# A two-layer diffusion trunk: channel sums of the last output tiles, idle products at the broadcasts, and the order of the residual update

## The chip, the cores and the metric

One core of one Trainium2 chip runs the whole program. The metric is the device time of one execution in microseconds, as the median of several runs.

## The reference

The model has two layers, and each layer three sublayers: a SwiGLU feed-forward, a token mixer with four branches, and a second feed-forward. There are 384 tokens (128 of a prompt, 256 latent ones) with 1024 channels. Every sublayer has the same frame, and the change lies in that frame:

```python
def trunk_layer(x, mod, lp, layer_idx, cache):
    h = modulate(x, lp["norm_pre"][0], mod[:, 0], mod[:, 1])
    x = residual_add(x, swiglu(h, lp["ffn_in"][0], lp["ffn_out"][0]), lp["norm_post"][0], mod[:, 2], 0.5)
...
def modulate(x, g_pre, shift, scale):
    return rms_norm(x, g_pre) * (1.0 + scale[:, None, :]) + shift[:, None, :]

def residual_add(x, y, g_post, gate, weight):
    return x + weight * gate[:, None, :] * rms_norm(y, g_post)
```

So at the end of a sublayer the mean of y^2 over the channels is needed for the update of x, and the mean of the new x^2 over the channels for the input h of the next sublayer. All arithmetic is float32.

## The kernel before

Channels lie on the partitions, tokens in the free dimension: x is eight tiles (KD = 8) of 128 channels by 384 tokens. Every float32 weight and activation is split into a rounded part and a rest (`split`, line 959: a CAST on ScalarE and a subtraction on VectorE or POOL), and each product is three products of the parts (`acc3`, lines 955 to 957). Weights come by DMA from SP into a ring of three and are split on arrival (`weight`).

A sublayer ends with eight output tiles. `out_evac` (line 991) takes each out of PSUM. Let c be the factor of a channel (weight, gate and norm_post together, one for the prompt's and one for the latent tokens, GRP). It makes y^2 (line 995, ScalarE, from PSUM), c y (line 1002, the tile `yp` or, in a mixer, `room`), (c y)^2 and x c y. The three squares and products are added over the tiles into `acc`, on POOL, some on VectorE in a mixer (line 1009). For tile 7 it makes x c y and (c y)^2 in two pieces directly from PSUM (lines 999 and 1000) and leaves them outside `acc`.

`sums` (line 1011) sums over the 128 channels of a tile on TensorE: a product with a column of ones, one per block of 128 tokens, nine for three tiles of 384 tokens. One such call takes `acc` (tiles 0 to 6) ahead of the last products of tile 7, another one, in `post_stats` (line 1020), the three tiles of tile 7. VectorE adds the two parts; `mp` (line 1033) is the mean of y^2, and POOL raises it to the power -1/2 (`qp`, line 1035). From the other sums, qp and the running mean of x^2, the mean of the new x^2 follows without a look at the new x (lines 1044 to 1048), and its power `qn` on POOL (line 1051).

`next_h` (line 1054) brings qp and qn to all partitions by three products each with the identity (`bcast`, line 968: Rp and Rn in PSUM), and then takes the eight tiles in turn: yp times Rp (line 1064), x plus that (line 1066, on VectorE for tile 0, on POOL for the others), xn = x times Rn (line 1074), h from xn on ScalarE in two pieces (line 1080), and its split. The first two weights of the next sublayer are loaded and split ahead (`self.early`); the second's rest (`lin`) is made in two halves by `rest` (line 945), whose place is fixed with `behind`, a dependency that only orders.

Beside this, products of the modulation's rows (line 855, "mod-row products": four products of 2 by 256 for each of eight row blocks) are placed there; `rows_gate` in `run` says behind which broadcast each block may stand. In the mixer the whole sublayer including its output tiles is recorded, and an order is computed by a planner with assumed costs (`Order`); it is emitted at line 1305, with idle products of a zero tile `wsrc` at line 1288 in TensorE's planned gaps. Outside the mixers the tile framework sets the order.

## Time and profile before

| what | us |
|---|---|
| median of 3 runs | 1970.43 |
| lowest and highest run | 1960.71, 1972.06 |
| the profiled execution, its time | 1969.64 |
| the profiled execution, its span | 1967.6 |
| TensorE busy in the span | 1885.2 |
| VectorE busy | 1230.4 |
| ScalarE busy | 825.4 |
| POOL busy | 428.4 |

The span goes from the first to the last instruction in the trace; the time of the execution holds some 2 us around it. In the rows below PE is TensorE's products, PEld its loading of weights, DVE is VectorE, ACT is ScalarE, POOL is GpSimd. A row of the timeline gives the start, the length, the engine, the line, the operation with the tiles it writes and reads, their shapes, how many equal instructions are merged, and in brackets how long the engine had waited and for whom. A float32 product of TensorE counts as two in the trace.

### The profile page before, as it was taken

Reading aid. Unit: us, or ns where it says so; the run is one execution under the profiler, and the core shown is the slowest. Engines: PE = TensorE matmul, PEld = TensorE weight load, DVE = VectorE, ACT = ScalarE, POOL = GpSimd, SP = SyncE. Lnnn points to the kernel's source line nnn. Section 1 sums busy time; section 2 is a strip of 40 time slices with the busy share of each in tenths; the row PEclk is TensorE's granted clock in tenths of the full one; section 3 lists DMA queues with packets and bytes.
Section 4 is the critical chain, followed back from the end, with each engine's and each line's share of the span. In section 5 each row is a group of like instructions: output and inputs, shape, how many; then the busy total and the mean of one; then the engine's idle time right before and its main releaser. Section 6 shows DMA issues by size and latency. Waiting matters only on the chain.

```text
span 1967.6 us, 36586 instructions
## 1 busy us (share of the span) xinstructions
PE 1885.2 (96%) x14962; PEld 1737.7 (88%) x14962; DVE 1230.4 (63%) x2272; ACT 825.4 (42%) x1463; POOL 428.4 (22%) x364
## 2 busy tenths in 40 slices
PE   6999999999999999999999999999999999999997
PEld 3989998888787879999979999978987778899997
DVE  3797476686678558635758735757866775433344
ACT  3433333565245453333353333344543544533332
POOL 0111132240100231121431111424100014222223
PEclk9999999989899989999999999999898999999999
DMA  9676454233231238635538644533333222333442
GB/s 368 204 245 209 142 189 159 97 90 90 70 98 60 97 117 278 200 124 162 162 137 276 205 129 154 170 104 95 83 95 77 84 91 81 102 125 124 126 125 91
DMA packets 118519, 277.15 MB, mean 141 GB/s; under 512 B 46416, under 2 KB 51792, under 8 KB 117968
## 3 DMA queue, kind: packets, MB, share of 16 engines
q1 hardware_dynamic: 70704, 252.75, 39.5%
q10 hardware_dynamic: 47648, 22.07, 4.5%
q8 instruction: 117, 1.92, 0.4%
q14 instruction: 50, 0.41, 0.1%
HBM read 266.92 MB, written 7.86 MB: 140 GB/s over the span
## 4 chain that ended last, share of the span: by engine, by line
PE 74%; DVE 13%; ACT 4%; issue 4%; DMA 3%; POOL 1%; ACTq 0%; DVEq 0%; POOLq 0%
PE psum L1305 23%; PE psum L956 16%; PE psum L957 16%; PE psum L955 16%; DVE room L1305 5%; DVE mj L822 3%; DVE lin L961 1%; ACT room L1305 1%; DMA mw<-in_wmod 1%; PE psum L1016 1%; DVE wlo L1305 1%; PE psum L968 1%; ACT whi L1305 1%; ACT h L1080 1%; DMA rfo<-in_ffn_out 1%
## 5 line engine op out<-in xcount | busy, mean ns | idle before, releaser
L957 PE MATMUL psum<-h,lin 128*128 128x384 f32 x1408 | 474.8, 337 | 13.3 <-DVE lin L961 13.3
L956 PE MATMUL psum<-h,hin 128*128 128x384 f32 x1408 | 475.6, 338 | 2.0 <-DVE h L961 1.5
L955 PE MATMUL psum<-h,hin 128*128 128x384 f32 x1408 | 470.0, 337 | 2.6 <-ACT h L960 2.0
L960 ACT CAST hin<-rin 128x1024 fp32r<-128x1024 f32 x175 | 183.9, 1052 | 401.7 <-PE psum L956 266.6
L961 DVE TENSOR_TENSOR lin<-rin,hin 128x1024 fp32r<-128x1024 f32 x175 | 217.2, 1242 | 175.1 <-ACT hin L960 175.1
L957 PEld LDWEIGHTS psum<-h,lin 128*128 128x128 f32 x1408 | 265.3, 188 | 19.6 <-DVE lin L961 19.4
L956 PEld LDWEIGHTS psum<-h,hin 128*128 128x128 f32 x1408 | 265.3, 188 | 9.0 <-DVE h L961 8.9
L961 POOL TENSOR_TENSOR hl<-hf,hh 128x384 fp32r<-128x384 f32 x88 | 137.7, 1564 | 613.9 <-ACT hh L960 613.9
L955 PEld LDWEIGHTS psum<-h,hin 128*128 128x128 f32 x1408 | 263.2, 188 | 7.5 <-ACT h L960 4.2
L822 DVE SCALAR_TENSOR_TENSOR mj<-mw,sr 128x1024 f32<-128x1024 f32 x176 | 250.8, 1425 | 16.4 <-DMA mw<-in_wmod 10.3
L1305 PE MATMUL psum<-room 32*32 32x32 f32 (+10 forms) x5112 | 241.8, 232 | 8.0 <-DVE room L1305 4.5
L1305 PEld LDWEIGHTS psum<-room 32*32 32x32 f32 (+5 forms) x5112 | 193.5, 132 | 56.6 <-issue 18.6
L957 PE MATMUL psum<-hh,lfo 128*128 128x384 f32 x704 | 237.6, 338 | 2.8 <-DVE lfo L961 2.8
L955 PE MATMUL psum<-hh,hfo 128*128 128x384 f32 x704 | 237.7, 338 | 1.9 <-ACT hfo L960 1.8
L956 PE MATMUL psum<-hl,hfo 128*128 128x384 f32 x704 | 236.9, 337 | 0.0
L1305 PE MATMUL psum<-h,whi 128*128 128x384 f32 x736 | 201.0, 353 | 6.3 <-ACT whi L1305 6.0
L960 ACT CAST hfo<-rfo 128x1024 fp32r<-128x1024 f32 (+1 forms) x96 | 94.1, 980 | 232.6 <-PE psum L956 167.2
L961 DVE TENSOR_TENSOR lfo<-rfo,hfo 128x1024 fp32r<-128x1024 f32 (+1 forms) x96 | 111.1, 1157 | 120.5 <-ACT hfo L960 120.5
L1009 POOL TENSOR_TENSOR acc<-acc,t 128x384 f32<-128x384 f32 x72 | 105.9, 1497 | 231.7 <-ACT t L995 231.7
L1305 PEld LDWEIGHTS psum<-h,whi 128*128 128x128 f32 x736 | 137.9, 196 | 11.0 <-ACT whi L1305 7.9
L957 PEld LDWEIGHTS psum<-hh,lfo 128*128 128x128 f32 x704 | 132.7, 188 | 4.9 <-DVE lfo L961 4.6
L955 PEld LDWEIGHTS psum<-hh,hfo 128*128 128x128 f32 x704 | 132.7, 189 | 3.2 <-ACT hfo L960 3.2
(189 smaller groups left out, 2508.7 us busy)
## 6 DMA issues: line engine op xcount, KB each, us to landing
rin<-in_ffn_in SPq DMA_DIRECT2D x176, 512.0 KB, 3.6
mw<-in_wmod SPq DMA_DIRECT2D x88, 512.0 KB, 4.6
rfo<-in_ffn_out SPq DMA_DIRECT2D x64, 512.0 KB, 3.6
wraw<-in_w_in SPq DMA_DIRECT2D x46, 512.0 KB, 3.6
rfo<-in_ffn_out SPq DMA_DIRECT2D x32, 384.0 KB, 3.2
m<-in_wmodk SPq DMA_DIRECT2D x16, 512.0 KB, 9.5
ma<-in_wmodk SPq DMA_DIRECT2D x16, 512.0 KB, 4.6
wraw<-in_w_out SPq DMA_DIRECT2D x16, 512.0 KB, 3.7
```

The source lines that it names most:

```text
L822: i = nc.vector.scalar_tensor_tensor(junk, w, 1.0, self.sr[:, c], op0=ALU.mult, op1=ALU.mult, accum_out=self.mod[l][:, part, j, c : c + 1])
L955: nc.tensor.matmul(ps, w, xh, start=first, stop=False)
L956: nc.tensor.matmul(ps, w, xl, start=False, stop=False)
L957: nc.tensor.matmul(ps, wl, xh, start=False, stop=last)
L960: return (self.nc.scalar.copy(hi, src), (engine or self.nc.vector).tensor_tensor(lo, src, hi.bitcast(F32), op=ALU.subtract))
L961: (engine or self.nc.vector).tensor_tensor(lo, src, hi.bitcast(F32), op=ALU.subtract))
L968: i = self.nc.tensor.matmul(ps[:, b * P : (b + 1) * P], r[:, b : b + 1].to_broadcast([P, P]), self.k("ident"), start=True, stop=True)
L1009: (nc.vector if (m, i) in quick else nc.gpsimd).tensor_tensor(acc[i], acc[i], t3[i], op=ALU.add)
L1016: self.summed = self.nc.tensor.matmul(st[:, 3 * i + b : 3 * i + b + 1], part[i][:, b * P : (b + 1) * P], self.k("ones")[:, 0:1], start=Tru ...
L1080: nc.scalar.activation(h[:, o : o + n], xn[:, o : o + n], AF.Identity, bias=B[:, j, g : g + 1], scale=A[:, j, g : g + 1])
L1305: getattr(getattr(nc, eng), n["fn"])(*args, **kw)
```

## The change

For tiles 6 and 7 `out_evac` now makes only y^2 (ScalarE) and x*y (VectorE, from PSUM over all 384 tokens), both without c. The factors come in where the channels are summed: the weight column is c for x*y, and for y^2 a pair of columns, 1 and c^2 (`w2`, made in `post_coef`), so that one product gives the sum of y^2 and that of (c y)^2. `acc` ends with tile 5. All sums go into the same nine columns of PSUM. The first call takes `acc` and tile 6, the second tile 7. At the end of the program only the sum of y^2 is taken. `warm` puts eight idle products behind the sums and, between two broadcasts, eight more. In `next_h` the update of tile j+1 (yp, x) stands ahead of xn of tile j, and the second half of `lin` behind the split of tile 1. `rows_gate` lets fewer row blocks stand ahead of the second broadcast.

```diff
@@ post_coef
+        self.w2 = self.one(f"w2{l}_{s}", [2, 2, 2], tag="w2", bufs=2)
+        nc.gpsimd.memset(self.w2[:, :, :, 0], 1.0)
+        nc.vector.tensor_tensor(self.w2[:, :, :, 1], c[:, KD - 2 :], c[:, KD - 2 :], op=ALU.mult)
@@ out_evac
+        late = m >= KD - 2
...
-        if m == KD - 1:
-            for g, (o, n) in enumerate(GRP):
-                nc.vector.scalar_tensor_tensor(t3[1][:, o : o + n], ps[:, o : o + n], c(g), self.x[:, m, o : o + n], op0=ALU.mult, op1=ALU.mult)
-                nc.scalar.activation(t3[2][:, o : o + n], ps[:, o : o + n], AF.Square, scale=c(g))
+        if late:
+            nc.vector.tensor_tensor(t3[1], self.x[:, m], ps, op=ALU.mult)
...
-                (nc.vector if (m, i) in quick else nc.gpsimd).tensor_tensor(acc[i], acc[i], t3[i], op=ALU.add)
+                nc.gpsimd.tensor_tensor(acc[i], acc[i], t3[i], op=ALU.add)
@@ sums
+    def sum_tile(self, st, m, t3, coef, only):
+        mm, stop = self.nc.tensor.matmul, False
+        both = st.rearrange("p (i b) -> p i b", b=3)[:, ::2]
+        for b in range(3):
+            g, blk = min(b, 1), slice(b * P, (b + 1) * P)
+            if only:
+                self.summed = mm(st[:, b : b + 1], t3[0][:, blk], self.k("ones")[:, 0:1], start=False, stop=m == KD - 1 and b == 2)
+            else:
+                mm(both[:, :, b], t3[0][:, blk], self.w2[:, m - KD + 2, g], start=False, stop=stop)
+        if not only:
+            for b in range(3):
+                g, blk = min(b, 1), slice(b * P, (b + 1) * P)
+                self.summed = mm(st[:, 3 + b : 4 + b], t3[1][:, blk], coef[:, m, g : g + 1], start=False, stop=m == KD - 1 and b == 2)
+
+    def warm(self, n):
+        ps = self.bank([P])
+        for _ in range(n):
+            self.behind(self.nc.tensor.matmul(ps, self.wsrc[:, :P], self.wsrc[:, :P], start=True, stop=True), self.gates[-1])
+        self.pf(ps)
@@ post_stats
-        for i in range(n):
-            nc.vector.tensor_scalar(cut(st, i), cut(acc[0], i), scale[i], 0.0 if i else EPS, op0=ALU.mult, op1=ALU.add)
-        st2 = self.sums(acc[1], n)
+        self.sum_tile(ps, KD - 1, t3, coef, last)
...
+        self.warm(8)
...
-        now = nc.vector.scalar_tensor_tensor(mp, cut(st2, 0), scale[0], cut(st, 0), op0=ALU.mult, op1=ALU.add)
+        now = nc.vector.tensor_scalar(mp, cut(ps, 0), 1.0 / D, EPS, op0=ALU.mult, op1=ALU.add)
@@ next_h
+        if Rp is not None and rn is not None:
+            self.warm(8)
...
+            if Rp is not None and (j == 0 or Rn is None):
+                ahead = step(j)
+            if Rp is not None and Rn is not None and j < KD - 1:
+                ahead = step(j + 1)
...
+            i = nc.vector.tensor_tensor(xn, self.x[:, j], Rn, op=ALU.mult)
+            if Rp is not None:
+                self.behind(i, ahead)
...
+            if Rp is not None and j == 1:
+                self.rest(self.made[1])
@@ run
-                self.rows_gate = {k: self.gates[(k + 1) // 2 - 1 if k < 7 else 2] for k in range(1, KD)}
+                self.rows_gate = {k: self.gates[0 if k == 1 else 1 if k < 4 else 2] for k in range(1, KD)}
@@ mix_out
-            t3 = self.out_evac(f"m{l}", m, ps, coef, yp, acc, ((5, 2), (6, 1), (6, 2)))
+            t3 = self.out_evac(f"m{l}", m, ps, coef, yp, acc)
```

TensorE's order at the end of the first mixer, before: the sums (128x1) of `acc`, then those of tile 7, the mod-row products (2x256) between them, and the broadcasts of qp and qn.

```order
L1305 MATMUL psum<-consts,room_2980 128x1 x9
L855 MATMUL psum<-room_2980,sc 2x256 x2
L1016 MATMUL psum<-consts,t_6855 128x1 x3
L855 MATMUL psum<-room_2980,sc 2x256 x2
L1016 MATMUL psum<-consts,t_6860 128x1 x3
L1016 MATMUL psum<-consts,t_6865 128x1 x3
L855 MATMUL psum<-room_2980,sc 2x256
L968 MATMUL psum<-consts,qp_6902 128x128 x3
L855 MATMUL psum<-room_2980,sc 2x256 x4
L968 MATMUL psum<-consts,qn_6913 128x128 x3
L855 MATMUL psum<-room_2980,sc 2x256 x23
```

The same place now, up to the first of the eight idle products (each is a LDWEIGHTS and a MATMUL of `wsrc`):

```order
L1335 MATMUL psum<-consts,room_2990 128x1 x9
L1335 MATMUL psum<-w_1_3007,t_6868 128x2 x3
L1335 MATMUL psum<-co_1_3006,t_6874 128x1 x3
L1029 MATMUL psum<-w_1_3007,t_6888 128x2 x3
L1033 MATMUL psum<-co_1_3006,t_6893 128x1 x3
L1039 LDWEIGHTS wsrc
L1039 MATMUL psum<-wsrc 128x128
```

And from the last idle product ahead of the second broadcast to the next sublayer's first products:

```order
L1039 LDWEIGHTS wsrc
L1039 MATMUL psum<-wsrc 128x128
L971 MATMUL psum<-consts,qn_6949 128x128 x3
L855 MATMUL psum<-room_2990,sc 2x256 x32
L958 MATMUL psum<-h_6965,hin_0_6909 128x384
```

The 21 sums now stand in one row, and all 32 mod-row products stand behind the second broadcast. After a feed-forward sublayer four of them stay ahead of the sums of tile 7 and 28 stand behind, where 23 stood.

VectorE's order in the first `next_h` behind a sublayer, before: yp is yp times Rp, `lin` the halves of the second early weight's rest, the row `h<-h` the split of tile 0.

```order
L1064 TENSOR_TENSOR yp_0_1957<-yp_0_1957,psum 128x384
L945 TENSOR_TENSOR lin_1_2818<-rin_1_2816,hin_1_2817 128x512
L1066 TENSOR_TENSOR x<-x,yp_0_1957 128x384
L945 TENSOR_TENSOR lin_1_2818<-rin_1_2816,hin_1_2817 128x512
L1074 TENSOR_TENSOR xn_0_2861<-x,psum 128x384
L1064 TENSOR_TENSOR yp_0_1957<-yp_0_1957,psum 128x384
L1064 TENSOR_TENSOR yp_1_1958<-yp_1_1958,psum 128x384
L1074 TENSOR_TENSOR xn_1_2870<-x,psum 128x384
```

Now:

```order
L1085 TENSOR_TENSOR yp_0_1960<-yp_0_1960,psum 128x384
L948 TENSOR_TENSOR lin_1_2818<-rin_1_2816,hin_1_2817 128x512
L1087 TENSOR_TENSOR x<-x,yp_0_1960 128x384
L1085 TENSOR_TENSOR yp_0_1960<-yp_0_1960,psum 128x384
L1100 TENSOR_TENSOR xn_0_2872<-x,psum 128x384
L1085 TENSOR_TENSOR yp_1_1961<-yp_1_1961,psum 128x384
L1100 TENSOR_TENSOR xn_1_2881<-x,psum 128x384
L1085 TENSOR_TENSOR yp_1_1961<-yp_1_1961,psum 128x384
L1100 TENSOR_TENSOR xn_2_2891<-x,psum 128x384
L964 TENSOR_TENSOR h_2867<-h_0_2873,h_2867 128x384
L1085 TENSOR_TENSOR yp_2_1962<-yp_2_1962,psum 128x384
L964 TENSOR_TENSOR h_2867<-h_1_2882,h_2867 128x384
```

A tile `yp_n` holds two of the eight tiles. The update of tile 1 moved ahead of xn_0, and the second half of `lin` from there to behind the split of tile 1 (it is the next row).

## Rows read from the trace of the kernel before

**Rows 1.** The page: busy time by engine, and the chain that ended last.

```profile
PE 1885.2 (96%) x14962; PEld 1737.7 (88%) x14962; DVE 1230.4 (63%) x2272; ACT 825.4 (42%) x1463; POOL 428.4 (22%) x364
...
PE 74%; DVE 13%; ACT 4%; issue 4%; DMA 3%; POOL 1%; ACTq 0%; DVEq 0%; POOLq 0%
```

**Rows 2.** Timeline, third place, 999 to 1011 us (start, length, engine, line, operation).

```profile
999.76 0.34 PE L957 MATMUL psum<-hh,lfo 128*128 128x384 f32 x1
...
1000.20 0.49 ACT L995 ACTIVATE t<-psum 128x384 f32<-128x384 f32 x1 [4.32 <-PE psum L957]
...
1000.80 0.35 DVE L999 SCALAR_TENSOR_TENSOR t<-psum,co,x 128x128 f32<-128x128 f32 x1 [2.46 <-ACT t L995]
...
1004.65 0.93 PE L968 MATMUL psum<-consts,qp 128*128 128x128 f32 x6 [0.67 <-POOL qp L1035]
...
1005.62 0.56 DVE L1064 TENSOR_TENSOR yp<-yp,psum 128x384 f32<-128x384 f32 x1 [0.24 <-PE psum L968]
...
1006.09 0.68 DVE L945 TENSOR_TENSOR lin<-rin,hin 128x512 fp32r<-128x512 f32 x1
...
1006.36 1.65 PE L968 MATMUL psum<-consts,qn 128*128 128x128 f32 x6
...
1006.69 0.55 DVE L1066 TENSOR_TENSOR x<-x,yp 128x384 f32<-128x384 f32 x1
...
1007.16 0.69 DVE L945 TENSOR_TENSOR lin<-rin,hin 128x512 fp32r<-128x512 f32 x1
...
1008.05 0.56 DVE L1074 TENSOR_TENSOR xn<-x,psum 128x384 f32<-128x384 f32 x1 [0.20 <-PE psum L968]
...
1010.19 0.55 DVE L1074 TENSOR_TENSOR xn<-x,psum 128x384 f32<-128x384 f32 x1 [0.66 <-POOL x L1066]
```

**Rows 3.** Windows, E to xn_0 at five places: length, busy times by engine, PEclk, DMA.

```profile
332.91:341.66 8.75, 7.70 (x61) 4.87 (x64) 3.92 (x14) 2.89 (x6) 1.72 (x2) 0.80 0.11 47
698.65:711.11 12.46, 12.14 (x71) 8.48 (x73) 4.79 (x19) 2.89 (x6) 1.71 (x2) 0.63 0.10 38
1000.10:1008.05 7.95, 6.79 (x52) 4.59 (x56) 4.01 (x14) 2.89 (x6) 1.71 (x2) 0.85 0.11 46
1297.11:1305.08 7.97, 6.81 (x53) 4.60 (x56) 4.00 (x14) 2.89 (x6) 1.71 (x2) 0.85 0.12 50
1659.50:1670.55 11.05, 10.73 (x71) 7.49 (x73) 4.79 (x19) 2.89 (x6) 1.71 (x2) 0.73 0.10 40
```

**Rows 4.** Windows, E to mp at the same five places.

```profile
332.91:336.67 3.76, 3.07 (x28) 2.36 (x28) 0.84 (x3) 2.19 (x6) 0.00 (x0) 1.00 0.27 109
698.65:705.73 7.08, 7.01 (x46) 5.56 (x45) 1.62 (x8) 2.89 (x6) 0.00 (x0) 0.73 0.18 67
1000.10:1003.50 3.40, 2.91 (x27) 2.28 (x28) 0.84 (x3) 2.19 (x6) 0.00 (x0) 1.00 0.27 107
1297.11:1300.51 3.40, 2.91 (x28) 2.29 (x28) 0.84 (x3) 2.19 (x6) 0.00 (x0) 1.00 0.29 117
1659.50:1665.17 5.67, 5.60 (x46) 4.57 (x45) 1.62 (x8) 2.84 (x6) 0.00 (x0) 0.94 0.19 77
```

**Rows 5.** Timeline of TensorE: sums, mod-row products, sums behind the first mixer, idle products.

```profile
327.62 2.07 PE L1016 MATMUL psum<-consts,acc 128*128 128x1 f32 x18
...
341.14 2.77 PE L855 MATMUL psum<-ma,sc 128*2 128x256 f32 x46
...
702.97 2.72 PE L1016 MATMUL psum<-consts,t 128*128 128x1 f32 x12
...
1320.72 0.62 PE L1288 MATMUL psum<-wsrc 128*128 128x128 bf16 x8
```

**Rows 6.** Windows, 703 to 710 us, behind the first mixer (columns as in rows 3).

```profile
703.00:710.00 7.00, 6.75 (x32) 4.73 (x31) 2.38 (x10) 1.36 (x3) 1.71 (x2) 0.50 0.01 2
```

**Rows 7.** Timeline: TensorE's waits in and behind the eight tiles of a next sublayer.

```profile
716.19 0.19 PEld L956 LDWEIGHTS psum<-h,hin 128*128 128x128 f32 x1 [0.40 <-DVE h L961]
...
1024.93 0.44 PE L957 MATMUL psum<-h,lin 128*128 128x384 f32 x1 [0.82 <-DVE lin L961]
```

More of the change, by code (lines that the diff above doesn't have):

```diff
@@ L1008, in out_evac, with sums @@
             for i in range(3):
-                (nc.vector if (m, i) in quick else nc.gpsimd).tensor_tensor(acc[i], acc[i], t3[i], op=ALU.add)
-    def sums(self, part, n=3):
+                nc.gpsimd.tensor_tensor(acc[i], acc[i], t3[i], op=ALU.add)
+    def sums(self, acc, t3, coef, only):
         st = self.bank([9])
-        for i in range(n):
+        for i in range(1 if only else 3):
             for b in range(3):
-                self.summed = self.nc.tensor.matmul(st[:, 3 * i + b : 3 * i + b + 1], part[i][:, b * P : (b + 1) * P], self.k("ones")[:, 0:1],
-                                                    start=True, stop=True)
-        return st
+                self.nc.tensor.matmul(st[:, 3 * i + b : 3 * i + b + 1], acc[i][:, b * P : (b + 1) * P], self.k("ones")[:, 0:1], start=i + b == 0, stop=False)
+        self.sum_tile(st, KD - 2, t3, coef, only)
+        return st
@@ L1026, in post_stats @@
         tiny = lambda x: self.one(f"{x}{nm}", [3], tag="tiny", bufs=6)
-        n = 1 if last else 3
-        for i in range(n):
-            nc.vector.tensor_scalar(cut(st, i), cut(acc[0], i), scale[i], 0.0 if i else EPS, op0=ALU.mult, op1=ALU.add)
-        st2 = self.sums(acc[1], n)
         self.gates = [self.summed]
+        self.warm(8)
         mp = tiny("mp")
-        now = nc.vector.scalar_tensor_tensor(mp, cut(st2, 0), scale[0], cut(st, 0), op0=ALU.mult, op1=ALU.add)
+        now = nc.vector.tensor_scalar(mp, cut(ps, 0), 1.0 / D, EPS, op0=ALU.mult, op1=ALU.add)
@@ L1036, in post_stats @@
         if last:
-            self.pf(acc[0], st2)
+            self.pf(ps)
             return rp, None
-        for i in (1, 2):
-            now = nc.vector.scalar_tensor_tensor(cut(st, i), cut(st2, i), scale[i], cut(st, i), op0=ALU.mult, op1=ALU.add)
-        self.pf(acc[0], st2)
+        st = self.one(f"st{nm}", [9], tag="stats", bufs=2)
+        for i, c in ((1, 2.0), (2, 1.0)):
+            now = nc.vector.tensor_scalar(cut(st, i), cut(ps, i), c / D, None, op0=ALU.mult)
+        self.pf(ps)
         self.rest(now)
@@ L1061, in next_h, with step @@
             hi, lo = self.halves(f"h{nm}")
[L1062 to L1068 removed]
+        def step(j):
+            i = nc.vector.tensor_tensor(yp[j], yp[j], Rp, op=ALU.mult)
+            quick = j == 0 if Rn is not None else j % 2
+            (nc.vector if quick else nc.gpsimd).tensor_tensor(self.x[:, j], self.x[:, j], yp[j], op=ALU.add)
+            return i
+        for j in range(KD):
+            if Rp is not None and (j == 0 or Rn is None):
+                ahead = step(j)
+            if Rp is not None and Rn is not None and j < KD - 1:
+                ahead = step(j + 1)
             if Rn is None:
@@ L1130, in ffn @@
                 if m == KD - 1 and k0 == 16:
-                    st = self.sums(acc, 1 if (l, s) == (DEPTH - 1, 2) else 3)
+                    st = self.sums(acc, t3, coef, (l, s) == (DEPTH - 1, 2))
                 wh, wl = self.weight(f"fo{nm}_{m}_{k0}", self.i["ffn_out"][l, w, m, :, k0 * P : (k0 + nk) * P], nk * P)
@@ L1353, in mixer @@
                    + [self.heads(l, h) for h in (0, 2)], self.lane_proj(l, hi, lo))
-        yp, (sums, t3) = self.mix_out(l, post)
+        yp, (sums, t3, coef) = self.mix_out(l, post)
         self.views.clear()
@@ L1365, in mixer @@
         self.rec = None
-        return yp, (st, t3)
+        return yp, (st, t3, coef)
     HSTEP = 1.0
```

25 lines of the change are left out of this document (8 added, 17 removed).

## The prediction

> **What bounds the kernel now.** I read the page first: TensorE is busy 96% of the span and carries 74% of the chain that ended last [rows 1]. So the long stretches of matrix products set the time, and only what lies between them can be gained without removing products. The change touches five such places, where one sublayer hands over to the next, and the end. Next I read the third of them (about 1000 us, feed-forward to feed-forward) in the timeline [rows 2]. The reader is to see one thread there: the last product of the sublayer starts at 999.76 and lasts 0.34, so it ends at 1000.10 (I call this E); ScalarE squares the output tile; VectorE and ScalarE then take turns on it; the first 1/rms input mp, the broadcasts, and at 1008.05 xn_0, from which the next sublayer's input is made, follow. Behind xn_0 a chain of ScalarE and VectorE work of fixed length per tile ends in the wait of TensorE at 1024.93 [rows 7]. I therefore take the start of xn_0 after E as the measure: what it comes earlier, the next sublayer ends earlier. After that I asked for the same stretch at all five places, once from E to xn_0 [rows 3] and once from E to mp [rows 4]; the bounds are read as at the third place. The first, third and fourth follow a feed-forward sublayer: 8.75, 7.95, 7.97 us, of which 3.76, 3.40, 3.40 up to mp. The second and fifth follow a mixer: 12.46 and 11.05, of which 7.08 and 5.67. The granted clock is 0.80 to 0.85 of full speed at the three and 0.63 and 0.73 at the mixers' two.
>
> **The change part by part.** *Tile 7 without factors.* Before, the tile's x*y is made in two pieces with the factor, in turns with two scaled squares on ScalarE, and mp waits for all eighteen sums. Now there is one Square, one x*y over 384 columns, then six sums. After a feed-forward sublayer: Square from E+0.10 for 0.49; x*y starts 0.11 behind it, as the product at 1000.80 did behind the square that ended at 1000.69 [rows 2], and lasts 0.56, the price of a product of 384 columns that reads PSUM (yp at 1005.62): E+1.26. On TensorE one sum of 128 channels costs 0.23, as nine of them took 2.07 [rows 5]. The trace does not have a sum with two output columns; it is no less than that one and no more than a broadcast product, 0.93/3 = 0.31 [rows 2], and I take 0.23, the nearer shape. Three sums of the squares start at E+0.64 and end at E+1.33, three of x*y end at E+2.02, mp follows at E+2.06. Against 3.76, 3.40, 3.40 that is 1.70 + 1.34 + 1.34 = 4.38 us. In the built program x*y waits for POOL as well, which reads tiles of the same ring; if that or VectorE held it back by as much as the two pieces took, the 4.38 would shrink to 0.
>
> *From mp to xn_0.* Before it is 4.99, 4.55, 4.57 at the three places and 5.38 twice at the mixers' (rows 3 less rows 4). At the third place the first broadcast took 0.93 and the second 1.65, and xn_0 waited 0.20 for the second [rows 2]: the clock had fallen between them. Now eight idle products stand before each broadcast. Eight took 0.62 [rows 5]; the first eight lie in the wait for the power on POOL (the 0.67 ahead of the broadcast, and the mod-row products that stood there before are moved behind), the second in the 0.78 between the end of the first broadcast (1005.58) and the second (1006.36), so I cost them at nothing; at half speed eight would take 1.24 and hold the second broadcast 0.46. If the clock holds, VectorE decides: yp at 1005.62, then steps of 0.47, 0.60, 0.47 (yp, half of lin, x, read from the starts), and now yp of tile 1 ahead of xn_0, 0.47 more: 1007.63, which is mp + 4.13. Gains: 0.86 + 0.42 + 0.44 = 1.72. Together the three feed-forward places give 6.10.
>
> *Mixers.* There no sum is early: the order puts nine sums of tiles 0 to 5, six of tile 6 and six of tile 7 all behind the last product, 21 in a row. At full speed they take 21 x 0.23 = 4.83, mp at E+4.87: a gain of 2.21 + 0.80. But the last six of eighteen took 2.72, or 0.45 each, at the second place [rows 5], in a stretch whose clock was 0.50 [rows 6]; with twelve at 0.45, mp stands at E+7.55 and 2.35 are lost. Then up to 1.25 each from mp to xn_0 if the clock holds there, nothing if not. So the two mixers give between -2.35 and 5.51; I take the middle, 1.6, as neither end has a row that is nearer.
>
> *Tile 6.* Its additions on POOL and one scaled square go, both beside products. But its six sums now stand on TensorE in front of the last eighteen products of tile 7: 6 x 0.23 = 1.38 at each of the three feed-forward places, in the middle of a stretch in which TensorE does not wait. That is 4.14 lost. At the end of the program three more sums stand there, 0.69. (At 0.31 each these are 5.6 and 0.9.)
>
> *Next tile's update ahead of xn.* xn_1 waited 0.66 for POOL's addition [rows 2]; with yp_1 done before xn_0 that wait goes, five times, 3.3. But the half of lin that stood before xn_0 (0.60) now stands behind lo_1, in the run of VectorE that feeds ScalarE. Net I take 0.06 x 5 = 0.3, with bounds of -3.0 and 3.3.
>
> *Mod-row products behind the second broadcast.* 23 (one is two rows of the trace) took 2.77 at the first place [rows 5]; now 28, and 32 behind a mixer, so 0.6 to 1.1 more. In the eight tiles that follow TensorE waits for the halves of each tile, 0.40 in the row shown [rows 7], which hides it; without that cover it would cost 4 us in all. The memsets and squares of coefficients for the sums are tiny and lie a sublayer ahead.
>
> *Sum.* 6.10 + 1.6 + 0.3 - 4.14 - 0.69 = 3.2 us earlier. The profiled execution took 1969.64, so 1966.4; I say 1966. That execution is 0.8 below the median of the three runs, which lie between 1960.71 and 1972.06; a measurement tells about 1%, 20 us, from no change.
>
> The Trainium skill (TensorE: Matmul & The Clock Gate, "What's actually happening") says that a busy TensorE is released to 2.4 GHz. The row does not agree as it stands: from 703 to 710 TensorE was busy 6.75 of 7.00 us, and the granted clock was 0.50, that is 1.2 GHz [rows 6]. By the page the idle products would hold the clock everywhere and the time would be that of the first rival; by the row a busy engine alone is no pledge of it.
>
> **The rivals.** *The clock holds at every broadcast and sum.* Then the mixers give 5.51 and the wait of xn_1 goes whole, 3.3: 6.10 + 5.51 + 3.3 - 4.83 = 10.1, or 1959.5. For it: the idle products fill just the gaps in which the clock fell. Against: 21 sums in a row at the mixers are longer than what stood there when it fell.
>
> *The clock falls behind the mixers and at the broadcasts, and the mod-row products decide.* This is the slower side. At half speed 28 of them cost 28 x 0.12 = 3.4 us more, all behind the second broadcast and ahead of the first product of the next sublayer; half of it is lost where ScalarE is the slower anyway, 1.7 x 5 = 8.5. With the sums at 0.45: 6.10 - 2.35 + 0.3 - 4.83 - 8.5 = -9.3, or 1979. It decides where the clock in the 7 us behind the second broadcast is below about 0.75.
>
> *Nothing left.* x*y of tile 7 comes no earlier than the two pieces did, since VectorE or POOL is behind; the 4.38 go: 1.72 + 1.6 + 0.3 - 4.83 = -1.2, or 1971. For it speaks that x*y waits for POOL as well; against it that POOL has three additions fewer just there.
>
> **How the numbers follow.** Forecast 0.45, clock holds 0.25, nothing left 0.15, slower side 0.10; 0.05 is for shifts inside the mixers, which these rows do not show. The range takes the forecast and the first and third case with some 6 us of run spread on either side: 1953 to 1977, which leaves out most of the slower side. Faster by over 1% (below 1950) needs twice the gain of the best case: 0.05. Slower by over 1% (above 1990): 0.03. Within 1%: 0.92.
>
> **What would show it.** Right: mp some 2.1 us behind E after a feed-forward sublayer and near 5 to 6 behind a mixer; both broadcasts at 0.93; xn_1 about 1.2 behind xn_0 in place of 2.14; eighteen products of tile 7 preceded by 15 sums in 3.45 us. Wrong: mp later than 3 us behind E, a clock of 0.5 at the broadcasts, the second broadcast held by idle products, or sums of tile 6 that wait for VectorE while TensorE stands.

## The result, and the profile after

The changed kernel takes 1977.09 us in the median of 8 runs (1971.28 to 1987.70); the kernel before took 1965.65 in 8 runs beside them. The ratio is 1.0060, with a 95% interval of 1.0035 to 1.0085: slower by some 11 us. The forecast of 1966 us, a small gain, was wrong in its sign, and the time lies 0.09 above the range.

The page of the changed kernel, the lines that answer to [rows 1] (its profiled execution took 1975.22, its span is 1973.4):

```profile
PE 1888.4 (96%) x15138; PEld 1756.6 (89%) x15138; DVE 1224.8 (62%) x2250; ACT 818.3 (41%) x1445; POOL 408.7 (21%) x358
...
PE 77%; DVE 12%; issue 4%; ACT 2%; DMA 2%; POOL 0%; ACTq 0%; DVEq 0%
```

TensorE is busy 3.2 us longer and carries 77% of the chain instead of 74%. So the loss is to be looked for in the stretches in which TensorE never stops.

The hand-overs themselves went much as forecast. The windows from E (end of the last main product) to xn_0 at the five places of the changed kernel, the answer to [rows 3]; the columns are length, then busy time and count of PE, PEld, DVE, ACT, POOL, then the granted clock, DMA share and GB/s:

```profile
338.67:344.98 6.31, 5.15 (x56) 3.98 (x60) 3.50 (x12) 2.16 (x4) 1.72 (x2) 1.00 0.01 1
695.14:704.61 9.47, 9.00 (x81) 8.28 (x85) 3.71 (x14) 2.77 (x6) 1.81 (x3) 0.82 0.19 56
1000.60:1007.62 7.02, 6.20 (x52) 5.23 (x56) 3.51 (x13) 2.15 (x4) 1.71 (x2) 0.76 0.01 2
1302.03:1308.34 6.31, 5.16 (x56) 3.98 (x60) 3.50 (x13) 2.15 (x4) 1.71 (x2) 1.00 0.00 0
1658.72:1671.40 12.68, 12.36 (x83) 10.49 (x85) 3.79 (x13) 2.77 (x6) 1.78 (x3) 0.64 0.12 41
```

Against 8.75, 12.46, 7.95, 7.97 and 11.05 [rows 3] that is 6.4 us less in all, even with the loss at the fifth place. The windows from E to mp, the answer to [rows 4]:

```profile
338.67:340.85 2.18, 2.08 (x24) 1.58 (x25) 0.56 (x2) 1.39 (x4) 0.00 (x0) 1.00 0.01 4
695.14:699.75 4.61, 4.61 (x45) 4.61 (x46) 0.76 (x2) 2.77 (x6) 0.10 (x1) 1.00 0.39 114
...
1302.03:1304.21 2.18, 2.08 (x24) 1.58 (x25) 0.56 (x2) 1.39 (x4) 0.00 (x0) 1.00 0.00 0
1658.72:1666.32 7.60, 7.60 (x54) 6.28 (x53) 0.76 (x2) 2.77 (x6) 0.00 (x0) 0.74 0.20 69
```

So the time was lost elsewhere. Laying the starts of ScalarE's casts of the two traces side by side shows where: ahead of E, in the second matrix of each feed-forward sublayer, and behind xn_0. Three things stand there.

**Ahead of E the clock falls.** The windows from the first sum ahead of E to E, at the three feed-forward places and at the end; first the kernel before (nine sums and eighteen products; at the end three sums):

```profile
327.62:332.91 5.29, 5.29 (x41) 5.04 (x44) 1.43 (x4) 1.05 (x1) 0.00 (x0) 1.00 0.68 225
994.80:1000.10 5.30, 5.30 (x41) 5.05 (x44) 1.43 (x4) 1.05 (x1) 0.00 (x0) 1.00 0.28 91
1291.82:1297.11 5.29, 5.29 (x41) 5.04 (x44) 1.43 (x4) 1.05 (x1) 0.00 (x0) 1.00 0.26 75
1950.33:1954.28 3.95, 3.95 (x25) 3.63 (x24) 0.16 (x1) 0.00 (x0) 0.00 (x0) 1.00 0.00 0
```

then the changed kernel (fifteen sums and eighteen products; at the end six sums):

```profile
328.86:338.67 9.81, 9.81 (x53) 9.56 (x56) 1.23 (x1) 1.04 (x1) 0.00 (x0) 0.65 0.35 137
990.79:1000.60 9.81, 9.81 (x53) 9.56 (x56) 1.22 (x1) 1.04 (x1) 0.00 (x0) 0.65 0.24 79
1293.81:1302.03 8.22, 8.22 (x53) 7.97 (x56) 1.23 (x1) 1.04 (x1) 0.00 (x0) 0.79 0.26 85
1955.01:1959.68 4.67, 4.67 (x31) 4.34 (x30) 0.00 (x0) 0.00 (x0) 0.00 (x0) 1.00 0.00 0
```

That is 4.52, 4.51, 2.93 and 0.72 more, 12.7 us. TensorE is busy in every one of these microseconds, yet the clock is at 0.65, 0.65 and 0.79. The timeline of TensorE at the first place in the changed kernel:

```profile
328.86 2.06 PE L1017 MATMUL psum<-consts,acc 128*128 128x1 f32 x18
330.79 1.11 PE L1029 MATMUL psum<-w,t 128*128 128x2 f32 x6
331.76 1.42 PE L1033 MATMUL psum<-co,t 128*128 128x1 f32 x6
333.04 0.67 PE L958 MATMUL psum<-hh,hfo 128*128 128x384 f32 x1
333.51 0.52 PE L959 MATMUL psum<-hl,hfo 128*128 128x384 f32 x1
333.83 0.52 PE L960 MATMUL psum<-hh,lfo 128*128 128x384 f32 x1
```

Nine sums take 2.06, as before. The clock falls in the second group (L1029, 1.11 for three sums); the third (L1033, six rows for three sums) takes 1.42, and the products behind it start 0.32 apart (333.51, 333.83) where they stood 0.17 apart: half clock, 1.2 GHz. In the kernel before, the clock fell behind E, by the second broadcast of [rows 2] (1.65 instead of 0.93), where TensorE waits for others as well; now it falls ahead of E, where every product pays.

**The products themselves are longer.** Six output tiles of the third sublayer (the second feed-forward one), ScalarE's square of one tile to that of the sixth behind it; the window of the kernel before:

```profile
918.81:987.46 68.65, 68.65 (x398) 68.61 (x397) 47.54 (x49) 26.86 (x44) 24.39 (x15) 1.00 0.55 175
```

and of the changed kernel:

```profile
913.63:983.32 69.69, 69.69 (x398) 69.69 (x397) 48.85 (x49) 26.82 (x43) 24.33 (x15) 1.00 0.55 172
```

The same 6 x 66 products, both at the full clock and without a gap, take 1.04 us more: 176.0 ns each instead of 173.3. (Such a product of two split parts is one row of the trace: 528 rows for 8 x 66 products in a whole sublayer. Two rows a product hold only for the sums, the broadcasts and the mod-row products.) Over 528 products in each of four sublayers that is 5.6 us, which no part of the prediction held.

**Behind xn_0 the tiles come later.** VectorE and POOL at the third place of the changed kernel:

```profile
1007.62 0.55 DVE L1100 TENSOR_TENSOR xn<-x,psum 128x384 f32<-128x384 f32 x1
...
1008.82 0.56 DVE L1100 TENSOR_TENSOR xn<-x,psum 128x384 f32<-128x384 f32 x1 [0.19 <-POOL x L1087]
...
1011.88 1.26 POOL L1087 TENSOR_TENSOR x<-x,yp 128x384 f32<-128x384 f32 x1 [0.96 <-DVE yp L1085]
1012.19 1.50 DVE L948 TENSOR_TENSOR lin<-rin,hin 128x512 fp32r<-128x512 f32 x1
1013.62 0.54 DVE L1100 TENSOR_TENSOR xn<-x,psum 128x384 f32<-128x384 f32 x1
```

xn_1 is 1.20 behind xn_0, as forecast, but the moved half of lin runs beside POOL's addition and takes 1.50 where it took 0.69 [rows 2], so xn_3 waits until 1013.62. In the kernel before POOL stood still there (1007.16), from its power to its first addition:

```profile
1005.46 0.85 POOL L1051 TENSOR_TENSOR qn<-mx,consts 128x3 f32<-128x3 f32 x1 [0.86 <-DVE mx L1048]
1009.14 1.98 POOL L1066 TENSOR_TENSOR x<-x,yp 128x384 f32<-128x384 f32 x2 [2.84 <-DVE yp L1064]
```

From xn_0 to xn_7 it is 11.57 now and was 10.57. The wait of TensorE for VectorE that ended at 1024.93 [rows 7], 24.83 behind E, now ends 25.06 behind E, although xn_0 came 0.93 earlier after E:

```profile
1025.66 0.44 PE L960 MATMUL psum<-h,lin 128*128 128x384 f32 x1 [1.04 <-DVE lin L964]
```

### The profile page after: what moved, and what is told of

Same layout as the page of the kernel before. It is cut to its first block, busy times and chain, and to the rows that moved or that the text cites. A ratio compares the mean times of both kernels' runs of the same rounds, so it can differ in the third digit from the quotient of the medians.

```text
span 1973.4 us, 36866 instructions
## 1 busy us (share of the span) xinstructions
PE 1888.4 (96%) x15138; PEld 1756.6 (89%) x15138; DVE 1224.8 (62%) x2250; ACT 818.3 (41%) x1445; POOL 408.7 (21%) x358
## 4 chain that ended last, share of the span: by engine, by line
PE 77%; DVE 12%; issue 4%; ACT 2%; DMA 2%; POOL 0%; ACTq 0%; DVEq 0%
PE psum L1335 26%; PE psum L959 16%; PE psum L960 16%; PE psum L958 16%; DVE room L1335 5%; DVE mj L822 2%; DVE lin L964 1%; ACT room L1335 1%; DVE h L964 1%; DMA mw<-in_wmod 1%; DVE wlo L1335 1%; DVE xn L1100 1%; DMA rfo<-in_ffn_out 1%; DVE lin L948 0%; PE psum L971 0%
## 5 line engine op out<-in xcount | busy, mean ns | idle before, releaser
L959 PEld LDWEIGHTS psum<-h,hin 128*128 128x128 f32 x1408 | 265.6, 189 | 11.0 <-DVE h L964 10.8
L1335 PE MATMUL psum<-room 32*32 32x32 f32 (+10 forms) x5112 | 236.9, 231 | 8.0 <-DVE room L1335 4.7
L1335 PEld LDWEIGHTS psum<-room 32*32 32x32 f32 (+5 forms) x5112 | 189.0, 131 | 55.7 <-issue 17.0
L959 PEld LDWEIGHTS psum<-hl,hfo 128*128 128x128 f32 x704 | 134.4, 191 | 0.0
```

What stands on the lines that cost most here:

```text
L959: nc.tensor.matmul(ps, w, xl, start=False, stop=False)
L1335: getattr(getattr(nc, eng), n["fn"])(*args, **kw)
```

## The experiments

The theory after this reading: three side effects eat the gain, (1) the place of hh and hl, moved by the new tile w2, (2) the run of fifteen small sums ahead of the last products, (3) the place of the half of lin. The rivals are named with each run. Times are medians beside runs of the kernel before on the same chip: 35 runs, median 1967.03, for b_shift64, a_shift128, a_six_late and a_lin_early; 23, 1965.23, for a_three_mended, a_spread, a_no_idle and a_rows_before; 22, 1965.67, for spread_no_idle and spread_old_order. A difference from the changed kernel is one of medians and is good to some 6 us, as the intervals of the two ratios tell.

### Only the place of hh and hl (b_shift64)

```diff
 # before: post_coef
+        self.one(f"pad{l}_{s}", [16], tag="pad", bufs=1)
         return c
```

> The kernel before, with one unused tile of 64 bytes per partition allocated behind the coefficients, so that every tile of the feed-forward hidden halves (hh, hl) and all behind them stand 64 bytes further, as in the changed kernel. Theory (placement): a product of the second feed-forward matrix costs 176.0 ns instead of 173.3, an output tile 11.62 us instead of 11.44, in all four feed-forward sublayers; the run is 4 to 5.5 us longer (ratio about 1.0025). Rival (what the changed kernel does beside these products slows them): 11.44 us a tile, ratio 1.000.

Measured: 1969.41 (12 runs), ratio 1.0018 (1.0000 to 1.0037). The six output tiles of this kernel, same window as above:

```profile
915.59:985.28 69.69, 69.69 (x398) 69.69 (x397) 47.44 (x49) 26.81 (x43) 24.40 (x15) 1.00 0.55 171
```

69.69, to the digit that of the changed kernel, from a tile that nothing writes or reads. The instructions are those of the kernel before; the place alone makes the products longer. The time bears it out only just: 2.4 us more, under the 4 to 5.5 expected, with an interval that begins at no change.

### A second 64 bytes in the changed kernel (a_shift128)

```diff
-        self.w2 = self.one(f"w2{l}_{s}", [2, 2, 2], tag="w2", bufs=2)
+        self.w2 = self.one(f"w2{l}_{s}", [2, 2, 4], tag="w2", bufs=2)[:, :, :, :2]
```

> The changed kernel with its new tile w2 made twice as large, so that hh, hl and all behind them stand 128 bytes further than before the change instead of 64. Nothing else differs. Theory (placement): an output tile takes 11.44 us again, the run is 4 to 5.5 us shorter than the changed kernel, about 1972. Rival (the changed work): 11.62 us a tile, no change from 1977.

Measured: 1973.62 (12 runs), ratio 1.0044 (1.0022 to 1.0066). In three sublayers the products are back at 173.3; in the first they stay at 175.8. Some 3.5 us less than the changed kernel, within the spread what three of four sublayers give (4.2), but the two intervals overlap: it is the products in the trace that show the place, not the time.

### Six sums behind E (a_six_late)

```diff
 # sums(), feed-forward sublayers only
-        self.sum_tile(st, KD - 2, t3, coef, only)
+        self.late6 = t3
 # post_stats()
+        self.sum_tile(ps, KD - 2, self.late6, coef, last)
         self.sum_tile(ps, KD - 1, t3, coef, last)
```

> The changed kernel; in the feed-forward sublayers the six sums of tile 6 stand behind the last product, ahead of those of tile 7, so that only nine sums stand before the last eighteen products, as before the change. Theory (the longer run of small sums lets the clock fall): the clock stays at 1.00 over the last eighteen products, these take 3.37 us instead of 5.63, 5.86 and 4.96, the nine sums 1.93; from the last product to mp 0.7 us more (2.9); together 8 to 10 us less than the changed kernel, about 1968. Rival (the clock falls there for another reason, as by the phase of the run): the eighteen products stay at 5 to 5.9 us, and the six sums only move: no change.

Measured: 1974.25 (12 runs), ratio 1.0041 (1.0021 to 1.0062); 2.8 less than the changed kernel, where 8 to 10 were expected, and the two intervals overlap. The mechanism came as expected: the window of nine sums and eighteen products ahead of the first E is

```profile
329.96:335.29 5.33, 5.33 (x40) 5.33 (x39) 1.22 (x1) 1.04 (x1) 0.00 (x0) 1.00 0.67 245
```

and the other two places read the same; mp moved to 3.24 behind E. But now the clock falls behind E again (6.8 us at half clock from E+3.7 at the first place), and the first product of the next sublayer comes 12.46 behind E there instead of 9.05. Moving the sums moves the fall; most of its price stays.

### The half of lin back behind x_0 (a_lin_early)

```diff
 # next_h, in step(j), behind the update of x
+            if Rn is not None and j == 0:
+                self.rest(add)
 # behind split of tile 1
-            if Rp is not None and j == 1:
-                self.rest(self.made[1])
```

> The changed kernel with the second half of lin back where it was, right behind the update of x in tile 0, instead of behind lo_1. Theory (that half, which took 1.50 us at 1012.19, holds xn_3 and so the chain of tiles): xn_0 about 0.5 later, from xn_0 to xn_7 10.6 instead of 11.6, the last wait of TensorE for VectorE 0.5 earlier at each of five places: 2 to 3 us less. Rival (the mod-row products behind the second broadcast decide): the first product of the next sublayer and that wait stay where they are, no change.

Measured: 1970.12 (12 runs), ratio 1.0015 (0.9995 to 1.0035): 7.0 less than the changed kernel, where 2 to 3 were expected. VectorE at the third place (E at 999.53):

```profile
1005.38 0.68 DVE L948 TENSOR_TENSOR lin<-rin,hin 128x512 fp32r<-128x512 f32 x1
...
1006.45 0.54 DVE L1102 TENSOR_TENSOR xn<-x,psum 128x384 f32<-128x384 f32 x1
...
1016.51 0.55 DVE L1102 TENSOR_TENSOR xn<-x,psum 128x384 f32<-128x384 f32 x1
```

The half takes 0.68, and xn_7 comes 10.06 behind xn_0 (11.57 in the changed kernel, 10.57 before). The wait for lin ends at 1023.02, 23.49 behind E instead of 25.06, that is 1.57 earlier. Not all of this is the half of lin: in the changed kernel's profile the clock had also fallen behind this E (xn_0 at 7.02). In a_shift128, which has the half in its new place, the clock stayed up there, xn_0 came 6.31 behind E (993.87), and the wait ended 24.35 behind it:

```profile
1018.22 0.44 PE L960 MATMUL psum<-h,lin 128*128 128x384 f32 x1 [1.03 <-DVE lin L964]
```

So the half is worth 0.86 at this place. That is 4.3 at five places if all are alike, which is not shown: at the first and the fourth, ahead of a mixer, there is no such wait. The rest of the 7.0 is not accounted for; the clock and the spread of the runs are large enough for it.

### All three mended (a_three_mended)

The last two edits, and the place of before given back:

```diff
-        st = self.one(f"st{nm}", [9], tag="stats", bufs=2)
+        st = self.one(f"st{nm}", [9], tag="stats", bufs=1)
```

> The changed kernel with three edits together: hh and hl stand where they stood before the change (the small statistics tile has one buffer instead of two, which gives back the 64 bytes of w2), the half of lin stands behind x of tile 0, and the six sums of tile 6 of the feed-forward sublayers stand behind the last product. Theory (these three are what made the change slower): 173.3 ns a product in all second feed-forward matrices, 3.37 us for the last eighteen products, 10.1 from xn_0 to xn_7, and a time of 1963 to 1967, no slower than before (ratio 0.997 to 1.001). Rival (something else in the change costs as well, as the 21 sums behind the mixers' last product or the mod-row products): 1970 or more.

Measured: 1959.95 (12 runs), ratio 0.9975 (0.9954 to 0.9995): faster than before, 17 us less than the changed kernel, and 3 below what the theory expected. Products 173.3 in all four sublayers, 3.37 for the last eighteen, 10.07 from xn_0 to xn_7. Nothing else in the change costs so much that the rival could stand. The three edits by themselves gave 3.5, 2.8 and 7.0; how the 17 divide among them the runs do not tell more closely than that. Behind E the clock still falls at all three feed-forward places.

### The sums one by one between the products (a_spread)

As a_three_mended, but the sums are handed out by a generator (left out here), one behind each three products:

```diff
-                if m == KD - 1 and k0 == 16:
+                if m == KD - 1 and k0 == 8:
                     st = self.sums(acc, t3, coef, (l, s) == (DEPTH - 1, 2))
...
                     self.acc3(ps, wh, wl, k, hid[k0 + k][0], hid[k0 + k][1], k0 + k == 0, k0 + k == KF - 1)
+                    for _ in range(2 if m == KD - 1 and k0 + k == 20 else 1):
+                        if self.due:
+                            next(self.due, None)
```

> As a_three_mended, but the fifteen sums of tiles 0 to 6 stand one by one between the products of tile 7, one behind each three products of the last fourteen channels, instead of nine in a row ahead of the last eighteen and six behind the last. Theory (it is the run of small sums in a row that lets the clock fall, not their number): the clock stays at 1.00 up to the last product, the fifteen cost 15 x 0.22 = 3.3 us or less there, from the last product to mp 2.2 instead of 3.2: 2 to 4 us less than a_three_mended, about 1962. Rival (the clock falls by the number of sums or by chance): half-clock products ahead of the last product as in the changed kernel, no gain.

Measured: 1957.30 (12 runs), ratio 0.9969 (0.9952 to 0.9985): the lowest median of all, 2.65 below a_three_mended, though the intervals of the two overlap. The window from the first sum to E at the first place, and then those from E to the first product of the next sublayer at the five places:

```profile
324.10:334.19 10.09, 10.09 (x70) 10.09 (x69) 3.66 (x7) 1.44 (x2) 0.00 (x0) 1.00 0.45 158
...
334.19:343.27 9.08, 8.02 (x107) 5.24 (x105) 6.07 (x17) 3.70 (x8) 3.69 (x4) 1.00 0.18 52
697.25:711.38 14.13, 13.52 (x134) 10.08 (x134) 8.19 (x21) 6.20 (x14) 4.79 (x6) 0.76 0.22 76
997.19:1006.27 9.08, 8.03 (x108) 5.25 (x106) 6.08 (x17) 3.71 (x8) 3.69 (x4) 1.00 0.17 57
1294.02:1303.09 9.07, 8.02 (x107) 5.25 (x105) 6.07 (x17) 3.70 (x8) 3.69 (x4) 1.00 0.18 61
1649.64:1664.44 14.80, 14.48 (x135) 11.32 (x134) 6.72 (x19) 4.77 (x11) 3.99 (x5) 0.77 0.24 69
```

The same fifteen sums, at 0.22 each, and the clock is 1.00 both ahead of E and behind it at the three feed-forward places. So it is small sums in a row, not their number, that go before the fall. At the mixers, where all 21 still stand in a row, the clock is 0.76 and 0.77.

One execution could be chance, as the rival has it, but the granted clock in all the traces says the same. Five kernels have fifteen sums in a row ahead of E (the changed one, a_shift128, a_lin_early, a_no_idle, a_rows_before): at 13 of their 15 feed-forward places the clock fell between the first sum and E. Three have them spread (a_spread, and spread_no_idle and spread_old_order below): at none of nine. Nine kernels have nine in a row (the one before, the six with the prefix b_, a_six_late, a_three_mended): at none of 27 ahead of E, but at all 27 within 6 us behind it; in the two with the sums spread and the idle products kept, at none of six within 10 us.

### Without the idle products (a_no_idle, spread_no_idle)

```diff
-        self.warm(8)          # post_stats
-        if Rp is not None and rn is not None:
-            self.warm(8)      # next_h
```

in the changed kernel:

> The changed kernel without the idle products (the eight behind the sums and the eight between the broadcasts). Theory (they hold the clock through the broadcasts): the second broadcast meets a clock of 0.50, from mp to xn_0 4.8 to 5.4 us at all five places instead of 4.13 to 5.08, 1 to 3 us more in all. Rival (the clock falls there by what stood earlier, and the idle products change nothing): mp to xn_0 as in the changed kernel, time the same within 2 us.

Measured: 1986.68 (6 runs), ratio 1.0110 (1.0088 to 1.0132), 9.6 us more than the changed kernel; and in a_spread:

> a_spread without the idle products. Theory (without them the clock falls in the hand-over): the low clock comes back behind the last product of the feed-forward sublayers, where a_spread has none, from the last product to the first of the next sublayer 10.5 to 12.5 us instead of 9.08, at the mixers 15 to 16 instead of 14.1 to 14.8; 6 to 10 us more than a_spread. Rival (the clock stays up by the spread sums alone): 9 us at the feed-forward places, the same time within 2 us.

Measured: 1968.13 (12 runs), ratio 1.0014 (0.9994 to 1.0033), 10.8 more than a_spread. So the idle products are worth about 10 us, more than either theory of the first run held. Where, the profile shows only in part: from E to the first product the feed-forward places were expected at 10.5 to 12.5 and came at 9.1 to 9.8. The windows from E to the first product without them:

```profile
335.73:345.56 9.83, 9.16 (x90) 5.38 (x90) 6.11 (x18) 3.75 (x8) 3.70 (x4) 0.83 0.15 47
696.37:710.95 14.58, 14.33 (x118) 9.68 (x118) 6.29 (x19) 4.34 (x10) 3.79 (x5) 0.77 0.22 61
998.58:1007.65 9.07, 7.77 (x90) 4.37 (x90) 6.07 (x17) 3.70 (x8) 3.68 (x4) 1.00 0.18 54
...
1659.14:1675.23 16.09, 15.84 (x119) 10.25 (x117) 7.69 (x20) 5.69 (x13) 4.68 (x5) 0.68 0.22 66
```

That is 0.75, 0.45, nothing and 1.29 more. The clock listed with each run makes up some of the rest: 2 x (1 - clock) x time, the time at half clock, is 112 us in the mean of these runs and 94 in those of a_spread. Which stretches these 18 us lie in is not settled. By the clock in the two profiles, that without the idle products has 12.9 us more at half clock, 10.2 of them within 20 us behind the five E (23.9 for 13.7). But a_no_idle and the changed kernel have 20.5 each in the same stretches, so those 9.6 us stay without a place.

### The gates of the mod-row products as before (a_rows_before)

```diff
-self.gates[0 if k == 1 else 1 if k < 4 else 2] for k in
+self.gates[(k + 1) // 2 - 1 if k < 7 else 2] for k in
```

> The changed kernel with the gates of the mod-row products as before the change (23 of them behind the second broadcast instead of 28, one between the two broadcasts, the rest ahead). Theory (TensorE waits for the halves of each tile there, which hides them): the first product of the next sublayer up to 0.6 earlier, the last wait for VectorE where it was, the time the same within 2 us of the changed kernel. Rival (they decide where the sublayer starts): 0.5 less at each of five places, 2.5 us in all.

Measured: 1982.86 (6 runs), ratio 1.0085 (1.0061 to 1.0109). The first product of the next sublayer comes 9.04 behind E at the first, third and fourth place, as at the first and fourth of the changed kernel (9.05, 9.04). So the five products more that now stand behind the second broadcast cost nothing there. The time is 5.8 above the changed kernel's, but the intervals overlap: no gain from undoing it, and whether it costs is open.

### VectorE's order in the hand-over as before (spread_old_order)

In a_spread, with next_h's loop as it was (yp, x, xn of a tile in turn):

> a_spread with the order of VectorE in the hand-over as before the change: yp, x and xn of one tile after the other, lin half behind x of tile 0. Theory (what the new order gains is the wait of xn_1 for POOL): xn_1 2.14 behind xn_0 instead of 1.20, from xn_0 to xn_7 10.57 instead of 10.06, from mp to xn_0 0.2 to 0.5 less; together 0 to 0.3 at each of five places, at most 1.5 us more than a_spread. Rival (the new order is worth its 0.9 at xn_1 in full): 4 us more.

Measured: 1961.17 (12 runs), ratio 0.9976 (0.9959 to 0.9994), against 0.9969 with the new order. The medians are 3.9 apart, near the rival's 4, but the intervals overlap, and the time does not decide. The trace does: with the old order xn_0 comes 0.46 earlier, xn_7 10.56 behind it, and the wait for lin at the third place ends 23.51 behind E, with the new order 23.50. At the second place the wait ends 26.71 and 26.65 behind E. So in the trace the order by itself is worth less than 0.1 at these places; what cost something is the half of lin that was moved with it.

### What about the place decides

Five single executions, all of the kernel before with tiles moved. In the first only what stands behind hh and hl moves by 64 bytes:

```diff
                 hh, hl = self.hid(f"hh{nm}_{f}", FR), self.hid(f"hl{nm}_{f}", FR)
+                if f == 0:
+                    self.sub.tile([P, 16], F32, tag="pad", bufs=1, name=f"pad{nm}")
```

> The kernel before with 64 unused bytes behind hh and hl: these stay where they are, yp, acc and what follows stand 64 bytes further. Theory (it is the place of hh and hl, which TensorE reads): 173.3 ns a product in all four second feed-forward matrices. Rival (the place of what other engines write meanwhile): 176.0.

The other four change the size of the unused tile of the first experiment (8, 48 and 64 elements for 32, 192 and 256 bytes), or put it of 64 bytes behind x instead, ahead of the weights:

> The kernel before with hh, hl and all behind them 32 bytes further, at a multiple of 64 bytes, where they were 32 off one before, and 32 off with the shift of 64 as well. Theory (it is a matter of alignment, and a multiple of 64 is good): 173.3 ns a product. Rival (it goes by the distance from the weights or by the particular place): 174 to 178.

> The kernel before with 64 unused bytes behind x, so that the weights, their halves, h, hh, hl and all that follows stand 64 bytes further and the distances between them stay. Theory (it is the distance of the moving tile from the weights): 173.3 ns a product of the second feed-forward matrix, as before. Rival (it is the place of hh and hl by itself): 176.0, as with hh and hl alone 64 bytes further.

> The kernel before with hh, hl and all behind them 192 bytes further. By the addresses, the remainder by 512 bytes of the distance from the weights to the moving tile is then 256, the same as that of h in the first matrix, which takes 173.3 in every run. Theory (the distance decides): 173.3 ns. Rival (only the place of before is good): 175 to 177.

> The kernel before with hh, hl and all behind them 256 bytes further. Theory A (what decides repeats every 256 bytes or fewer): 173.3 ns as at the old place. Theory B (it repeats every 512 bytes or not at all): anything from 173.3 to 177; together with the shifts of 0, 32, 64, 128 and 192 this says which distances are free.

By the program's allocation hh starts at byte 98016 of a partition in the kernel before and the weights' halves at 50336; hh's other tiles follow in multiples of 512 bytes, the weights' in multiples of 512 too. So one number, the distance between them modulo 256, holds for all products of a matrix. The times are means of the steps from one product's start to the next at the full clock, waits left out:

| kernel | distance mod 256 | ns a product, first / other three sublayers |
|---|---|---|
| before; b_shift_behind; b_all64; b_shift256 | 64 | 173.4 or 173.3 / 173.3 |
| b_shift32 | 96 | 176.6 / 176.7 |
| b_shift64; the changed kernel | 128 | 175.8 or 175.7 / 176.0 |
| a_shift128 | 192 | 175.8 / 173.3 |
| b_shift192 | 0 | 173.6 / 173.3 to 173.4 |
| h in the first matrix, every run | 0 | 173.5 to 173.6 |

The two that tell address from distance, six output tiles each; all tiles moved together by 64:

```profile
921.22:989.86 68.64, 68.64 (x398) 68.60 (x397) 47.39 (x49) 26.88 (x43) 24.33 (x15) 1.00 0.56 174
```

and hh, hl and what follows moved to a multiple of 64 bytes (b_shift32):

```profile
916.47:986.43 69.96, 69.96 (x398) 69.96 (x397) 48.16 (x49) 26.84 (x44) 24.33 (x15) 1.00 0.54 170
```

The address by itself does not decide: with hh at the slow address but the weights moved along, the product is as short as before. Nor does alignment: at a multiple of 64 bytes it is the longest. That it is the distance from the weights is the likeliest reading, since of the tiles ahead of hh these products read only the weights; no run moved the weights alone. Why the distance of 192 is slow in the first sublayer and not in the others stays open. The times of these five (1973.27 and 1978.92 for b_shift_behind and b_shift32; 1975.32, 1968.38 and 1968.57 for the three others, beside 1972.13 for one execution of the kernel before) are of one execution each and say nothing here.

## Why the prediction was wrong

- **Tile 7 without factors: right.** Forecast 2.06 from E to mp, measured 2.18, 2.17, 2.18; a gain of 4.0 for 4.38.
- **From mp to xn_0: right at two of three.** Forecast 4.13; 4.13 at the first and fourth place, 4.85 at the third, where the clock had fallen (0.76). A gain of 1.0 for 1.72.
- **Mixers: right in sum, by luck.** E to xn_0 3.0 shorter at the second place and 1.6 longer at the fifth: 1.4 for the 1.6 taken. The middle came out because the two places fell to the two ends: from E to mp 4.61 at the second, where the clock held (forecast 4.87), and 7.60 at the fifth, where it fell (forecast 7.55).
- **Tile 6: the size was right, the clock was left out.** "6 x 0.23 = 1.38 at each of the three" holds where the clock does: at the last place three sums cost 0.72, and in a_shift128's fourth place, where the clock stayed up, the stretch took 1.34 more. In the changed kernel it took 12.0 at the three for 4.14, and in the mean of the five profiles with this row 9.1, of which the sums themselves are some 4.0. The prediction asked of the clock only behind E and at the broadcasts; its slower rival had the clock as its cause, but put the fall behind the second broadcast. This is the step that failed most: six more sums "in the middle of a stretch in which TensorE does not wait" were priced at the full clock, and behind the longer row the clock fell and the eighteen products paid for it.
- **Next tile's update: failed.** "Net I take 0.06", bounds -3.0 and 3.3; xn_7 came 1.00 later behind xn_0, and undoing the move of the half of lin gave 7.0 in the medians, 0.86 at the third place in the traces. The wait of xn_1 went as forecast and was worth nothing in the trace (spread_old_order). The half was priced at 0.60 from a row where POOL stands still; beside POOL's addition it took 1.50, in VectorE's run for ScalarE. With it fell the measure itself: the chain behind xn_0 was taken to be "of fixed length per tile", but the change put work into it, and at the third place xn_0 came 0.93 earlier and the wait ended 0.23 later.
- **Coefficients for the sums: failed.** "The memsets and squares of coefficients for the sums are tiny", and so they were put at nothing: the instructions are tiny, but the tile they write moved hh and hl. By the products 5.6 us at most; alone, in b_shift64, 2.4 (ratio 1.0000 to 1.0037).
- **Mod-row products hidden: right** by the start of the next sublayer.
- **Idle products: the cost right, the gain too low.** "I cost them at nothing" holds at the third place: the wait for lin ends 24.35 behind E with them (a_shift128) and 24.35 without (a_no_idle), though the first product comes 9.04 with them and 8.61 without. Their gain was held to lie from mp to xn_0, 1.72 and up to 2.5 at the mixers; the runs give about 10 us, and where they lie is open. Without them the change would have been slower by 1.1%.

In the two profiles the differences add up, as they must when the marks leave nothing out: -6.4 from E to xn_0, +12.7 ahead of E, +4.7 by the place (1.4 in three sublayers, 0.5 in the first, where TensorE also waits for transfers), +4.7 behind xn_0 in the three feed-forward sublayers that follow a hand-over, +1.1 at the start and the end, -10.9 inside the mixers (xn_0 to E, 350.2 and 350.4 for 357.0 and 354.4): 5.9 for the 5.8 by which the span is longer. The medians are 11.4 apart. Part of the mixers' gain is the luck of this execution: in the mean of the ten profiles with the changed mixers these stretches take 352.1 and 351.6, of the seven with the old ones 355.9 and 353.3. What in the mixers gives these 5 us was not tried. The fall ahead of E was dearer in this execution too, 12.0 for the mean of 9.1.

## What to carry to other kernels

Price every edit in the stretches where the busiest engine never waits before those where it does: there, in this kernel, 2.7 ns on a product, or half a clock for 6 us, was paid in full. After any change of buffers compare the time of one unchanged product in both traces; a small new tile can shift large ones behind it. And be wary of small products in a row ahead of large ones: spread here, one behind each three large ones, they cost 0.22 each as in a row, and the clock did not fall. Last, an instruction moved to another place has another price there: ask what the other engines do beside it.

## What the runs showed of the hardware

- **A busy TensorE is no pledge of the clock.** 9.81 us busy of 9.81, and a clock of 0.65, behind fifteen sums with one or two columns in a row; 1.00 with the same sums spread out. The Trainium skill (TensorE: Matmul & The Clock Gate, "What's actually happening") has activity release the clock; the trace does not agree as it stands, for TensorE was active in all of these 9.81 us. That the fall follows the sums was shown in these places, at 13 of 15; in a_shift128 two of three such rows went without one.
- **The spread of the runs goes with the clock.** Over 35 runs of the kernel before, the time rises 0.36 us for each us at half clock (98 to 146 us a run, from the clock and time listed with each), and a straight line leaves 1.4 of the spread's 4.5 us (both standard deviations). In the two other sets, of 23 and 22 runs, it is 0.33 and 0.31.
- **VectorE beside POOL.** The subtraction of 128x512 took 1.50 beside an addition on POOL, at all five places of the changed kernel, and 0.68 without. The Trainium skill (SBUF — State Buffer, "SBUF: two separate sides") says that the two engines share a port pair as an exclusive lock, also where VectorE has two inputs in SBUF and GpSimd reads SBUF, and that the one that comes second is blocked. The trace comes near it: POOL's addition had begun 0.31 earlier and ran on for 0.95, and the subtraction took 0.82 longer. A shorter case does not fit: POOL's power of three columns (1005.46, 0.85) ran on for 0.21 beside the first half of lin [rows 2], which took 0.68 all the same.
- **The moving tile's place against the weights** was worth up to 3.4 ns on 173.3 in a product of 384 columns (176.7 in b_shift32). The same section of the Trainium skill says that TensorE waits for no other engine at SBUF; no run here speaks against that, for b_shift64 and b_all64 have the same instructions on every engine and differ only in where tiles stand.
